# Decay rows of a DeltaNet kept as one DRAM row per head and direction, with their loads and the S5 input store on ScalarE's queue

## The chip, the cores and the metric

The kernel runs on one core of a Trainium2 chip. A core has TensorE (matmuls; its weight loads are shown apart, as PEld), VectorE (DVE), ScalarE (ACT), GpSimd (POOL) and SyncE (SP). Each takes its instructions strictly in order, and they wait for each other on semaphores. DMA transfers are issued as instructions of an engine's queue, here mostly SP's and some ScalarE's; sixteen DMA engines then move the data. [...] 

The metric is the time of one execution on the device in microseconds (us), the median of the runs. The profile is of one execution.

## The reference

One inference step of a hybrid backbone: two layers (DEPTH = 2), 512 latent and 128 context tokens (640 in all), width 1024, float32. Each layer normalises its input, projects it once, and splits the columns among three mixers: a long convolution (Hyena), a diagonal state space model (S5) and a gated DeltaNet with 8 heads of 128 x 128 state in both directions. Each output is gated and projected, the three are merged, and the result is added to the input. Cut to the part whose data the change moves, the DeltaNet takes the tokens in chunks:

```python
gc = jnp.cumsum(g, axis=-1)                       # log decays, within a chunk
diff = gc[..., :, None] - gc[..., None, :]
decay = jnp.where(lower, jnp.exp(jnp.where(lower, diff, 0.0)), 0.0)
a_mat = jnp.where(strict, jnp.einsum('bhncd,bhnsd->bhncs', kb, k) * decay, 0.0)
t_mat = lax.linalg.triangular_solve(a_mat + eye, ...)    # the inverse
...
qk = jnp.where(lower, jnp.einsum('bhncd,bhnsd->bhncs', q, k) * decay, 0.0)
...
    v_new = u_i - jnp.einsum('bhcd,bhdv->bhcv', w_i, S)
    o = (jnp.einsum('bhcd,bhdv->bhcv', q_i * jnp.exp(g_i)[..., None], S)
         + jnp.einsum('bhcs,bhsv->bhcv', qk_i, v_new))
```

The kernel does this in five blocks of 128 tokens; `a_mat` is its tile `N`, `qk` its tile `Pm`. For `decay`, every head and direction needs the row of `gc` of its 640 tokens on all 128 partitions, against the column of each partition.

## The kernel before

Activations are kept transposed: channels on partitions, 640 tokens along the row. Every float32 matmul is done as three faster ones on operands that are split in a high and a low part: `split` (L68) makes `wh` with a cast on ScalarE (L69) and `wl` with a subtraction on VectorE or GpSimd (L70), and `mm3` (L87) runs the three products (L91). `load_w` (L77) loads a 128 x 512 piece of weights, `wr`, on SP (L81), a few pieces ahead. TensorE's projections go on as long as `wr`, `wh` and `wl` arrive in time.

`run` goes over the two layers. In a layer come the norm, then S5 in eight column blocks and the Hyena convolution side by side, then the DeltaNet (`gdn`, L1026), then the merge. Matmuls of gates (results `pg`, sums `gst`, stored to `gt`) are spread between as filler.

S5, `s5_in` (L834): the projection of a block is copied to `u` by ScalarE (L844, L845), stored to the DRAM tile `us` (L846), and read back in another layout by eight loads `U<-us` (L882), which TensorE uses at L908.

DeltaNet: `gdn_scalars` (L1071) computes the running log decays `gc`, 128 tokens x (5 blocks x 16), turns them into `gr` with 80 rows of 128 (L1126), row b * 16 + c for block b and head and direction c, and stores them to the DRAM tile `gcd` (L1127). Then the eight heads go in pairs. `gdn_front` (L1132) projects q, k and v of a head through the gated convolution (`gx`, `gy`, `QT`, `KT`), and makes `kn` and `v`. `gdn_pairs` (L1195) loads, for each of two directions, the 640 values of g of its head onto all 128 partitions (L1202, tile `Pm`, 320 KB), five VectorE operations subtract the column (L1206, through the helper at L138), ScalarE takes the exponential (L1207), and the products with k k and q k follow on VectorE (`N`, `Pm`). `gdn_inverse` (L1313) inverts the triangular `N` of two heads in a chain of VectorE steps (`lt`, `Yl`, L1335 and L1336) and builds `YD`, `YT`, `YB`, `Y1T` from it. `gdn_scan` (L1230) runs the chunks; TensorE reads `Pm` there last (L1253).

Two pools of two buffers each hold `Pm`, so four heads are in work: at a layer's DeltaNet start eight loads of `Pm` come in one burst, after that groups of four.

The order of the instructions on each engine is set when the kernel is built: a scheduler with a simulated timeline picks the next ready instruction from all loops. Where a DMA is issued, what it waits for and how long the simulation takes it to last all enter, so an edit of a DMA can move other instructions.

Of the kernel before, what the change touches and what calls it, by code (L numbers as in the profile page):

```python
# [12 lines left out]
F32 = mybir.dt.float32  # L13
# [39 lines left out]
def bc(ap, shape):  # L53
    return ap.to_broadcast(shape)


class Net:
# [776 lines left out]
    def s5_in(self, l, ct, p, T):  # L834

        nc, a = self.nc, self.a
# [5 lines left out]
        u = p.tile([128, 8, 82], F32, name="u", tag="ys")  # L842
        nc.gpsimd.memset(u[:, :, 64:82:17], 0.0)
        nc.scalar.copy(u[:, :, 0:64], Pu[:, 0:NLAT].rearrange("p (j t) -> p t j", t=8))  # L844
        nc.scalar.copy(u[:, :, 65:81], Pu[:, NLAT:].rearrange("p (j t) -> p t j", t=8))  # L845
        nc.sync.dma_start(T["us"][ct * 128:(ct + 1) * 128], u)  # L846

        ld = {}
        for n in ("sbr", "sbi"):
# [176 lines left out]
    def gdn(self, l, P):  # L1026
        tc, nc, a = self.tc, self.nc, self.a
        self.q2 = self.proj_pools(P, "n", nc.gpsimd, NPM)
        self.pm = P(name="pmb", bufs=NPU, space=PSUM)

        pa = P(name="gda", bufs=1)
        ph = [P(name="gdb", bufs=2)]
        cp = self.gcp
        c = cp.tile([128, 2, 128], F32, name="c6")
        nc.sync.dma_start(c, a["c128"][:, 384:].rearrange("p (n c) -> p n c", n=2))
        self.tri = c
        self.gcw = cp.tile([128, 24, 3], F32, name="gcw")
        nc.scalar.dma_start(self.gcw, a["gcw"][l].rearrange("p (n c) -> p n c", n=24))
        self.ngh = cp.tile([128, 1], F32, name="ngh")
        nc.scalar.dma_start(self.ngh, a["gng"][l])  # L1040
        self.gcd = self.dp.tile([80, 128], F32, name="gcd%d" % l)
        with self.pool(name="gdt", bufs=1) as p:
            self.gdn_scalars(l, cp, p)
        pi = P(name="gdi", bufs=1)
        ph.append(P(name="gdd", bufs=2))
        p = P(name="gdp", bufs=1)

        def front(h):
            return [self.gdn_front(l, h + i, pa, ph[h // 2 % 2]) for i in range(2)]

        def pairs(h, f):
            for i in range(2):
                self.gdn_pairs(h + i, ph[h // 2 % 2], f[i])

        self.LD = pi.tile([128, 32, 32], F32, name="LD")
        nc.gpsimd.memset(self.LD, 0.0)
        self.Y1 = None
        f = front(0)
        pairs(0, f)
        for h in range(0, 8, 2):  # L1060
            self.gdn_inverse(pi, f)
            self.gdn_scan(l, h, p, f)
            if h < 6:
                f = front(h + 2)
                pairs(h + 2, f)
# [5 lines left out]
    def gdn_scalars(self, l, cp, p):  # L1071

        nc, a = self.nc, self.a
        raw = p.tile([128, KT, 32], F32, name="wbr")
        nc.sync.dma_start(raw, a["wba"][l].rearrange("p (k c) -> p k c", k=KT))
        wh = p.tile([128, KT, 32], F32R, name="wbh")
        wl = p.tile([128, KT, 32], F32R, name="wbl")
        self.split(wh, wl, raw)
        ba = p.tile([32, NTOK], F32, name="ba")
        for h in range(2):  # L1080
            s = slice(h * 320, h * 320 + 320)
            P = self.half()
            for kh in range(2):
                self.mark = self.mm3(P[:32], kh, wh[:, 4 * kh:4 * kh + 4], wl[:, 4 * kh:4 * kh + 4], self.hh, self.hl, s, m=32)
            nc.scalar.copy(ba[:, s], P[:32])
        pt = self.half(512)
        for b in range(5):
            self.tr(pt[:, b * 32:b * 32 + 32], ba[:, b * 128:(b + 1) * 128])
        bt = p.tile([128, 5, 32], F32, name="bt")
        nc.vector.tensor_copy(bt, pt[:, :160].rearrange("p (b c) -> p b c", b=5))  # L1090
        al = p.tile([128, 16], F32, name="alog")
        nc.scalar.dma_start(al, bc(a["alog"][l], [128, 16]))
        nc.gpsimd.tensor_tensor(al, self.ebase[:, :16], al, op=ALU.pow)
        dtb = p.tile([128, 16], F32, name="dtb")
        nc.scalar.dma_start(dtb, bc(a["dtb"][l], [128, 16]))
        sh = [128, 5, 16]
        T = lambda n: p.tile(sh, F32, name=n)
        C = lambda n: cp.tile(sh, F32, name=n)
        beta = C("beta")
        nc.scalar.activation(beta, bt[:, :, 0:16], AF.Tanh, scale=0.5)  # L1100
        self.ts(nc.vector, beta, beta, 0.5, 0.5)
        x, ax, g = T("gx"), T("gax"), T("gg")
        nc.vector.tensor_tensor(x, bt[:, :, 16:32], bc(dtb.unsqueeze(1), sh), op=ALU.add)

        nc.scalar.activation(ax, x, AF.Abs)
        nc.scalar.activation(ax, ax, AF.Tanh, scale=0.5)
        self.ts(nc.vector, ax, ax, 0.5, 0.5)
        nc.scalar.activation(ax, ax, AF.Ln)
        self.stt(x, x, 0.0, ax, ALU.max, ALU.subtract)
        self.stt(g, x, -1.0, bc(al.unsqueeze(1), sh))  # L1110
        pc = self.half(512)
        for d in range(2):
            nc.tensor.matmul(pc[:, d * 40:d * 40 + 40], self.tri[:, d, :], g[:, :, d * 8:d * 8 + 8], start=True, stop=True)
        nc.tensor.matmul(pc[:, 128:208], self.ones, g, start=True, stop=True)
        gc = C("gc")
        for d in range(2):
            nc.vector.tensor_copy(gc[:, :, d * 8:d * 8 + 8], pc[:, d * 40:d * 40 + 40].rearrange("p (b c) -> p b c", b=5))
        tot = pc[:, 128:208].rearrange("p (b c) -> p b c", b=5)
        egl, dec, neg, pos = C("egl"), C("dec"), C("neg"), C("pos")
        nc.scalar.activation(egl, tot, AF.Exp)  # L1120
        nc.vector.tensor_tensor(dec, tot, gc, op=ALU.subtract)
        nc.scalar.activation(dec, dec, AF.Exp)
        pr = self.half(512)
        self.tr(pr[:80, :128], gc.rearrange("p b c -> p (b c)"))
        gr = p.tile([80, 128], F32, name="gr")
        nc.scalar.copy(gr, pr[:80, :128])  # L1126
        nc.sync.dma_start(self.gcd, gr)  # L1127
        nc.scalar.activation(pos, gc, AF.Exp)
        self.ts(nc.vector, neg, pos, -1.0)
        self.gs = dict(beta=beta, egl=egl, dec=dec, neg=neg, pos=pos, gc=gc)  # L1130
# [64 lines left out]
    def gdn_pairs(self, h, p, x):  # L1195

        nc, G, KT, QT = self.nc, self.gs, x["KT"], x["QT"]

        Pm = p.tile([128, 2, 5, 128], F32, name="Pm")
        Ed = [Pm[:, d] for d in range(2)]  # L1200
        for d, E in enumerate(Ed):
            nc.sync.dma_start(E, bc(self.gcd.rearrange("(b c) i -> c b i", b=5)[d * 8 + h:d * 8 + h + 1],  # L1202
                                    [128, 5, 128]))
            for b in range(5):
                g = G["gc"][:, b, d * 8 + h:d * 8 + h + 1]
                self.ts(nc.vector, E[:, b, :], E[:, b, :], g, g, ALU.min, ALU.subtract)  # L1206
            nc.scalar.activation(E, E, AF.Exp)  # L1207
        N = p.tile([128, 2, 5, 128], F32, name="N")
        for b0 in (0, 2, 4):
            pb = self.half(512)  # L1210
            n = min(2, 5 - b0)
            pv = pb[:, :n * 256].rearrange("p (x b c) -> p x b c", x=2, b=n)
            for b in range(n):
                t = slice((b0 + b) * 128, (b0 + b) * 128 + 128)
                nc.tensor.matmul(pv[:, 0, b, :], KT[:, t], KT[:, t], start=True, stop=True)
                nc.tensor.matmul(pv[:, 1, b, :], KT[:, t], QT[:, t], start=True, stop=True)
            for d in range(2):
                for b in range(n):
                    self.stt(N[:, d, b0 + b, :], pv[:, 0, b, :], x["sk"][:, b0 + b, d:d + 1], Ed[d][:, b0 + b, :])
                nc.vector.tensor_tensor(Pm[:, d, b0:b0 + n, :], pv[:, 1], Ed[d][:, b0:b0 + n, :], op=ALU.mult)  # L1220

        nc.gpsimd.memset(N[64:128, 0, :, 0:64], 0.0)
        nc.gpsimd.memset(N[0:64, 1, :, 64:128], 0.0)
        for q in (0, 64):
            nc.gpsimd.memset(N[q + 32:q + 64, 0, :, q:q + 32], 0.0)
            nc.gpsimd.memset(N[q:q + 32, 1, :, q + 32:q + 64], 0.0)
        nc.gpsimd.tensor_tensor(Pm, Pm, bc(self.tri.unsqueeze(2), [128, 2, 5, 128]), op=ALU.mult)
        x.update(N=N, Pm=Pm)
# [470 lines left out]
```

## Time and profile before

| | |
|---|---|
| median of 3 runs | 3738.56 us (3723.69 to 3741.91) |
| profiled execution | 3732.11 us |
| its span, first to last instruction | 3730.3 us |
| mean granted TensorE clock | 0.95 |
| TensorE busy | 3380.0 us, 91% of the span |
| VectorE, GpSimd, ScalarE busy | 64%, 52%, 38% |
| `Pm<-gcd` loads | 32 of 320 KB, landing after 11.0 us (median) |
| `us<-u` stores | 16 of 328 KB, landing after 4.2 us (median) |

Engine rows read thus: time, engine, line, operation, output tile <- input tiles, shape, how many alike. In square brackets stands how long the engine was idle just before, and whose end released it. A duration with SPq is the time for which SP was busy issuing, not the transfer; the transfer's end is the landing. Busy time of a matmul is modelled from its issue, and at the lower clock the same matmul takes longer, so a stretch is judged by busy time and granted clock together.

### The profile page before, as it was taken

To read this page: it belongs to the slowest core of one execution; us is meant where nothing else is said; L and a number is where in the kernel's file an instruction comes from. 1 tells how busy PE (TensorE), PEld (TensorE's weight loads), DVE (VectorE), ACT (ScalarE), POOL (GpSimd) and SP (SyncE) were. 2 spreads that over 40 slices of the span, in tenths; PEclk is the share of its full clock that TensorE was granted. 3 is DMA by queue.
4 is the path that set the end of the run, shared out by engine and by line. 5 is a ranking of instruction groups with operands and counts; after the bars stand their busy time and mean duration, and the time that the engine had idled before them with its cause. 6 is when DMAs were issued, how large, how long until landed. Compare 5 with 4: busy or idle time off the path is not lost. (4 is left out here: it accounts for less than half of the span.)

```text
span 3730.3 us, 68509 instructions
## 1 busy us (share of the span) xinstructions
PE 3380.0 (91%) x25850; PEld 3220.4 (86%) x25850; DVE 2369.6 (64%) x4615; ACT 1413.4 (38%) x3295; POOL 1942.9 (52%) x2153
## 2 busy tenths in 40 slices
PE   6899898999979898899979999999989898898998
PEld 5798878888979887799978889988889898797998
DVE  6777677777227873743747776677773378875354
ACT  4433232332244445443334333323322545445422
POOL 4777777776345443401336777878763544341010
PEclk7999899999989998999989999999999999899999
DMA  6322334322232212533633222233222322134352
GB/s 242 110 73 82 94 107 115 108 73 63 78 93 65 68 62 68 170 126 109 188 113 98 75 71 83 81 75 81 76 66 77 92 64 78 41 97 139 125 178 89
DMA packets 310602, 363.05 MB, mean 97 GB/s; under 512 B 86814, under 2 KB 190270, under 8 KB 310016
## 3 DMA queue, kind: packets, MB, share of 16 engines
q1 hardware_dynamic: 305368, 358.01, 32.6%
q8 instruction: 204, 3.34, 0.4%
q10 hardware_dynamic: 4904, 0.66, 0.1%
q14 instruction: 126, 1.03, 0.1%
HBM read 291.87 MB, written 66.67 MB: 96 GB/s over the span
## 5 line engine op out<-in xcount | busy, mean ns | idle before, releaser
L91 PE MATMUL pj<-hh,wh 128*128 128x320 f32 x2048 | 666.4, 326 | 60.5 <-ACT wh L69 32.2
L91 PE MATMUL pj<-hh,wl 128*128 128x320 f32 x2048 | 655.5, 322 | 10.5 <-DVE wl L70 8.0
L91 PE MATMUL pj<-hl,wh 128*128 128x320 f32 x2048 | 657.9, 321 | 5.5 <-DVE hl L70 5.4
L70 POOL TENSOR_TENSOR wl<-wr,wh 128x512 fp32r<-128x512 f32 x288 | 392.1, 1365 | 448.9 <-ACT wh L69 388.7
L69 ACT CAST wh<-wr 128x512 fp32r<-128x512 f32 x608 | 374.8, 618 | 659.7 <-PE pj L91 486.3
L91 PEld LDWEIGHTS pj<-hh,wh 128*128 128x128 f32 x2048 | 400.7, 196 | 70.8 <-ACT wh L69 33.6
L91 PE MATMUL pg<-hh,wh 128*128 128x320 f32 x1280 | 415.1, 325 | 15.2 <-ACT wh L69 10.5
L91 PE MATMUL pg<-hh,wl 128*128 128x320 f32 x1280 | 407.6, 323 | 9.3 <-POOL wl L70 9.2
L70 DVE TENSOR_TENSOR wl<-wr,wh 128x512 fp32r<-128x512 f32 x320 | 259.5, 812 | 244.4 <-ACT wh L69 243.1
L91 PEld LDWEIGHTS pj<-hh,wl 128*128 128x128 f32 x2048 | 398.8, 195 | 14.9 <-DVE wl L70 9.3
L91 PE MATMUL pg<-hl,wh 128*128 128x320 f32 x1280 | 411.5, 322 | 0.0
L91 PEld LDWEIGHTS pj<-hl,wh 128*128 128x128 f32 x2048 | 400.3, 195 | 11.1 <-DVE hl L70 8.8
L91 PE MATMUL pj<-yh,wh 128*128 128x320 f32 x1024 | 318.0, 312 | 6.5 <-ACT yh L69 5.1
L91 PE MATMUL pj<-yl,wh 128*128 128x320 f32 x1024 | 318.9, 312 | 2.6 <-DVE yl L70 2.5
L91 PE MATMUL pj<-yh,wl 128*128 128x320 f32 x1024 | 317.5, 311 | 0.0
L91 PEld LDWEIGHTS pg<-hh,wh 128*128 128x128 f32 x1280 | 250.4, 196 | 19.4 <-ACT wh L69 11.6
L91 PEld LDWEIGHTS pg<-hh,wl 128*128 128x128 f32 x1280 | 247.4, 194 | 14.2 <-POOL wl L70 12.5
L91 PEld LDWEIGHTS pg<-hl,wh 128*128 128x128 f32 x1280 | 249.5, 195 | 0.9 <-issue 0.4
L91 PEld LDWEIGHTS pj<-yh,wh 128*128 128x128 f32 x1024 | 193.4, 189 | 8.1 <-ACT yh L69 5.9
L91 PEld LDWEIGHTS pj<-yl,wh 128*128 128x128 f32 x1024 | 193.5, 189 | 4.8 <-DVE yl L70 4.8
L91 PEld LDWEIGHTS pj<-yh,wl 128*128 128x128 f32 x1024 | 193.6, 189 | 0.0
L1514 POOL TENSOR_TENSOR m<-m,gt 128x640 f32<-128x640 f32 x16 | 31.1, 1943 | 295.8 <-DVE gt L132 295.8
(523 smaller groups left out, 8673.3 us busy)
## 6 DMA issues: line engine op xcount, KB each, us to landing
wr<-in_wt SPq DMA_DIRECT2D x608, 256.0 KB, 2.7
gt<-gst SPq DMA_DIRECT2D x160, 160.0 KB, 2.0
gt<-gt SPq DMA_DIRECT2D x64, 320.0 KB, 3.4
wr<-in_wmod SPq DMA_DIRECT2D x64, 256.0 KB, 3.3
Pm<-gcd SPq DMA_DIRECT2D x32, 320.0 KB, 11.0
wm<-in_wmod SPq DMA_DIRECT2D x4, 2048.0 KB, 16.8
M<-ks SPq DMA_DIRECT2D x256, 32.0 KB, 1.8
us<-u SPq DMA_DIRECT2D x16, 328.0 KB, 4.2
```

Of the source, the lines that this page charges most:

```text
L69: self.nc.scalar.copy(h, src)
L70: (eng or self.nc.vector).tensor_tensor(l, src, h.bitcast(F32), op=ALU.subtract)
L91: ins = self.nc.tensor.matmul(o, w[:, k, :m], x[:, kh * 4 + k, s], start=kh == 0 and k == 0 and i == 0, stop=kh == 1 and k == 3 and i == 2)
L1514: nc.gpsimd.tensor_tensor(m[i], m[i], g, op=ALU.add)
```

## The change

There are three edits. The S5 input store (L846) is issued from ScalarE's queue and not from SP's. The DRAM tile `gcd` gets the shape 16 x 5 x 128, so that the 640 values of one head and direction lie in one row of 2560 bytes; the store at L1127, still on SP, writes its 80 rows of 512 bytes to their new places. The 32 loads at L1202 read such a row as one run for each partition, where they read five runs of 512 bytes that lay 8 KB apart, and they are issued from ScalarE's queue.

```diff
--- before.py
+++ after.py
@@ -843,7 +843,7 @@
         nc.gpsimd.memset(u[:, :, 64:82:17], 0.0)
         nc.scalar.copy(u[:, :, 0:64], Pu[:, 0:NLAT].rearrange("p (j t) -> p t j", t=8))
         nc.scalar.copy(u[:, :, 65:81], Pu[:, NLAT:].rearrange("p (j t) -> p t j", t=8))
-        nc.sync.dma_start(T["us"][ct * 128:(ct + 1) * 128], u)
+        nc.scalar.dma_start(T["us"][ct * 128:(ct + 1) * 128], u)
 
         ld = {}
         for n in ("sbr", "sbi"):
@@ -1038,7 +1038,7 @@
         nc.scalar.dma_start(self.gcw, a["gcw"][l].rearrange("p (n c) -> p n c", n=24))
         self.ngh = cp.tile([128, 1], F32, name="ngh")
         nc.scalar.dma_start(self.ngh, a["gng"][l])
-        self.gcd = self.dp.tile([80, 128], F32, name="gcd%d" % l)
+        self.gcd = self.dp.tile([16, 5, 128], F32, name="gcd%d" % l)
         with self.pool(name="gdt", bufs=1) as p:
             self.gdn_scalars(l, cp, p)
         pi = P(name="gdi", bufs=1)
@@ -1124,7 +1124,7 @@
         self.tr(pr[:80, :128], gc.rearrange("p b c -> p (b c)"))
         gr = p.tile([80, 128], F32, name="gr")
         nc.scalar.copy(gr, pr[:80, :128])
-        nc.sync.dma_start(self.gcd, gr)
+        nc.sync.dma_start(self.gcd.rearrange("c b i -> b c i"), gr)
         nc.scalar.activation(pos, gc, AF.Exp)
         self.ts(nc.vector, neg, pos, -1.0)
         self.gs = dict(beta=beta, egl=egl, dec=dec, neg=neg, pos=pos, gc=gc)
@@ -1199,8 +1199,7 @@
         Pm = p.tile([128, 2, 5, 128], F32, name="Pm")
         Ed = [Pm[:, d] for d in range(2)]
         for d, E in enumerate(Ed):
-            nc.sync.dma_start(E, bc(self.gcd.rearrange("(b c) i -> c b i", b=5)[d * 8 + h:d * 8 + h + 1],
-                                    [128, 5, 128]))
+            nc.scalar.dma_start(E, bc(self.gcd[d * 8 + h:d * 8 + h + 1], [128, 5, 128]))
             for b in range(5):
                 g = G["gc"][:, b, d * 8 + h:d * 8 + h + 1]
                 self.ts(nc.vector, E[:, b, :], E[:, b, :], g, g, ALU.min, ALU.subtract)
```

The lines below the edit at L1202 are one lower in the changed kernel (the exponential is at L1206, `N` copies at L1380).

ScalarE at the DeltaNet start of layer 0, from the copy that fills the stored rows on; `wh<-wr` is the weight cast, `gx<-pj` a projection's copy. Before:

```order
L1126 COPY gr<-pj 80x128
L69 CAST wh<-wr 128x512
L1147 COPY gx<-pj 128x320
L1207 ACTIVATE Pm<-Pm 128x640
L69 CAST wh<-wr 128x512
L1147 COPY gx<-pj 128x320
```

After:

```order
L1126 COPY gr<-pj 80x128
L1202 DMA Pm<-gcd_10377 128x640 x3
L69 CAST wh<-wr 128x512
L1202 DMA Pm<-gcd_10377 128x640 x3
L1147 COPY gx<-pj 128x320
L1202 DMA Pm<-gcd_10377 128x640 x2
L1206 ACTIVATE Pm<-Pm 128x640
L69 CAST wh<-wr 128x512
```

The eight loads stand among the casts and copies; the exponentials and casts keep their order.

SP at the same place; `wr<-in_wt` are weight loads, `gt<-gst` stores of gates. Before:

```order
L81 DMA wr<-in_wt 128x512
L1127 DMA gcd_10377<-gr 80x128
L1202 DMA Pm<-gcd_10377 128x5x128 x8
L81 DMA wr<-in_wt 128x512 x3
L1425 DMA gt_496<-gst 128x320
```

After:

```order
L81 DMA wr<-in_wt 128x512
L1127 DMA gcd_10377<-gr 5x16x128
L81 DMA wr<-in_wt 128x512 x3
L1424 DMA gt_496<-gst 128x320
L81 DMA wr<-in_wt 128x512 x4
```

The weight loads follow the store directly, and the store's outermost size is 5 where it was 80.

VectorE at the last group of four loads in layer 1, around the first operations on `Pm`; `YD`, `YT`, `YB`, `Y1T` and `N` are tiles of the inverse of the heads in work, `S` and `os` of the scan, `fac` of the output gate. Before:

```order
L1185 TENSOR_TENSOR kn<-pj,dec 128x512 x2
L138 TENSOR_SCALAR fac<-fac 128x5
L1336 TENSOR_TENSOR Yl<-Yl,lt 128x31
L138 TENSOR_SCALAR Pm<-Pm,gc 128x128 x5
L1257 COPY S_32709<-pb 128x128
L138 TENSOR_SCALAR Pm<-Pm,gc 128x128
L1342 STREAM_TRANSPOSE YD<-Yl 128x1024
L138 TENSOR_SCALAR Pm<-Pm,gc 128x128 x2
```

After:

```order
L1352 STREAM_TRANSPOSE YB<-YD 128x160
L1351 STREAM_TRANSPOSE YT<-YD 128x160
L1352 STREAM_TRANSPOSE YB<-YD 128x160
L1270 TENSOR_TENSOR os_32461<-os_32461,pb 128x128
L1380 COPY N<-YB 32x10x32 x2
L1374 COPY Y1T<-YT 32x10x32 x4
L1380 COPY N<-YB 32x10x32 x6
L1185 TENSOR_TENSOR kn<-pj,dec 128x512 x2
L138 TENSOR_SCALAR Pm<-Pm,gc 128x128 x3
```

Before, the operations on `Pm` stand ahead of the transpose `YD`; after, `YD` and all that is made from it stand ahead of them. TensorE's own order is the same over most of layer 1; in layer 0's S5 and Hyena stage rows have moved by up to a hundred places.

## Rows read from the trace of the kernel before

**Rows 1.** Page, part 1: busy us, share of the span, instructions of each engine.

```profile
PE 3380.0 (91%) x25850; PEld 3220.4 (86%) x25850; DVE 2369.6 (64%) x4615; ACT 1413.4 (38%) x3295; POOL 1942.9 (52%) x2153
```

**Rows 2.** Windows: length, busy PE, PEld, DVE, ACT, POOL; PEclk, DMA share, GB/s.

```profile
1025.00:1055.00 30.00, 13.04 (x56) 12.12 (x55) 12.05 (x42) 10.47 (x17) 5.45 (x5) 0.66 0.44 106
1285.00:1300.00 15.00, 8.55 (x43) 8.55 (x44) 10.85 (x28) 9.27 (x17) 5.16 (x6) 0.77 0.53 118
1420.00:1450.00 30.00, 16.35 (x98) 14.95 (x102) 9.89 (x37) 12.90 (x25) 9.40 (x10) 0.71 0.36 99
2885.00:2915.00 30.00, 19.33 (x100) 18.54 (x100) 13.70 (x44) 15.79 (x24) 6.76 (x6) 0.77 0.54 128
3120.00:3145.00 25.00, 17.25 (x87) 15.88 (x85) 16.12 (x53) 11.55 (x32) 7.92 (x9) 0.73 0.42 116
3240.00:3265.00 25.00, 14.58 (x76) 13.68 (x75) 17.74 (x53) 12.12 (x26) 8.39 (x10) 0.69 0.36 85
100.00:950.00 850.00, 774.35 (x6035) 721.03 (x6035) 609.07 (x975) 271.77 (x762) 632.73 (x740) 0.95 0.34 91
1950.00:2800.00 850.00, 789.02 (x5872) 750.38 (x5871) 605.88 (x907) 281.81 (x768) 644.49 (x736) 0.97 0.30 79
```

**Rows 3.** Line L1202: issue ns min/median/max, who waited for it (us, times), landing.

```profile
L1202 SPq DMA_DIRECT2D Pm<-gcd x32: 371/517/4936, 1017.6 to 3245.9; - x32
...
  DVE Pm L138: 86.8, 23
...
DMA to landing us min/median/max: 7.8/11.0/15.4
```

**Rows 4.** Timeline of SP at both DeltaNet starts: start us, us, what.

```profile
1017.61 18.59 SPq L1202 DMA_DIRECT2D Pm<-gcd  x8
1036.30 15.77 SPq L81 DMA_DIRECT2D wr<-in_wt  x3
...
2878.61 14.32 SPq L1202 DMA_DIRECT2D Pm<-gcd  x8
2893.02 13.55 SPq L81 DMA_DIRECT2D wr<-in_wt  x3
```

**Rows 5.** Timeline of TensorE, 1025 to 1055 us, the two longest waits.

```profile
1030.12 0.63 PE L91 MATMUL pj<-hh,wh 128*128 128x320 f32 x1 [3.78 <-ACT wh L69]
...
1050.40 0.63 PE L91 MATMUL pj<-hh,wh 128*128 128x320 f32 x1 [12.74 <-ACT wh L69]
```

**Rows 6.** Timeline of ScalarE, same stretch.

```profile
1028.82 0.74 ACT L1207 ACTIVATE Pm<-Pm 128x640 f32<-128x640 f32 x1 [8.76 <-DVE Pm L138]
...
1049.73 0.62 ACT L69 CAST wh<-wr 128x512 fp32r<-128x512 f32 x1 [9.61 <-DMA wr<-in_wt]
```

**Rows 7.** Timeline of VectorE, 1420 to 1450 us, the two longest waits.

```profile
1422.94 0.60 DVE L138 TENSOR_SCALAR Pm<-Pm,gc 128x128 f32<-128x128 f32 x2 [7.35 <-DMA Pm<-gcd]
...
1442.18 1.37 DVE L138 TENSOR_SCALAR Pm<-Pm,gc 128x128 f32<-128x128 f32 x5 [9.38 <-DMA Pm<-gcd]
```

**Rows 8.** Chain that ended last, 3120 to 3260 us: start us, us, step.

```profile
3131.66 9.34 DMA Pm<-gcd
```

**Rows 9.** Line L1506, loads of `m` in the merge: issue ns, landing us.

```profile
L1506 SPq DMA_DIRECT2D m<-md x16: 320/430/997, 1641.9 to 3453.4; - x16
...
DMA to landing us min/median/max: 3.0/6.1/7.3
```

**Rows 10.** Page, part 6: DMA issues, KB each, us to landing.

```profile
fg<-in_fg SPq DMA_DIRECT2D x1, 512.0 KB, 4.1
...
gcd<-gr SPq DMA_DIRECT2D x2, 40.0 KB, 1.5
```

**Rows 11.** Line L695, loads that ScalarE issues: issue ns min/median/max.

```profile
L695 ACTq DMA_DIRECT2D stp<-in_ls x4: 473/473/487, 45.3 to 1795.2; - x4
```

**Rows 12.** Line L846, the S5 input store: landing.

```profile
DMA to landing us min/median/max: 2.2/4.2/8.8
```

**Rows 13.** Line L882, loads of the S5 input: who waited (us, times).

```profile
  PE pb L908: 12.8, 5
```

## The prediction

> **What bounds the kernel now.** I read the busy times first. TensorE is busy for 3380.0 of 3730.3 us, no other engine for more than 64% [rows 1], so the end moves only where TensorE gets work sooner. Next I cut the span into stretches and took for each its length less TensorE's busy time multiplied by its granted clock share: the time lost to gaps and to the slow clock together. Over 1950 to 2800 us that is 850 - 789.02 x 0.97 = 85 us, about 1 us in 10; it is the kernel's usual level. Six stretches are much worse, and in all six the Decay rows (tile Pm) are being loaded [rows 2]:
>
> | stretch, us | lost | usual | excess |
> |---|---|---|---|
> | 1025 to 1055 (GDN start, layer 0) | 30 - 13.04 x 0.66 = 21.4 | 3.0 | 18.4 |
> | 2885 to 2915 (GDN start, layer 1) | 30 - 19.33 x 0.77 = 15.1 | 3.0 | 12.1 |
> | 1285 to 1300 | 15 - 8.55 x 0.77 = 8.4 | 1.5 | 6.9 |
> | 1420 to 1450 | 30 - 16.35 x 0.71 = 18.4 | 3.0 | 15.4 |
> | 3120 to 3145 | 25 - 17.25 x 0.73 = 12.4 | 2.5 | 9.9 |
> | 3240 to 3265 | 25 - 14.58 x 0.69 = 14.9 | 2.5 | 12.4 |
>
> The excess is 75.1 us: 30.5 at the two starts, 44.6 in the four middle stretches. That is all there is to win near these loads.
>
> Then I asked what is late there. The 32 Pm loads land 7.8 to 15.4 us after issue, median 11.0; VectorE waits for them 86.8 us in 23 places [rows 3]. At a GDN start SP spends 18.59 us (layer 1: 14.32) issuing eight of them, and the three weight loads queued behind take another 15.77 (13.55) [rows 4]. The effect on TensorE is two gaps, 3.78 us and 12.74 us, both ended by the cast `wh` [rows 5]. The two have different causes. The first cast stands in ScalarE's queue behind the exponential of the first Pm, which waited 8.76 us for VectorE; the second waited 9.61 us for the weight load itself [rows 6]. In the middle stretches (four loads each) VectorE stands still, 7.35 and 9.38 us in the worst one [rows 7], and two such loads lie on the chain that ended last, one with 9.34 us [rows 8].
>
> **The change part by part.**
>
> *The load's shape.* A load reads 128 runs of 2560 B where it read 640 runs of 512 B. No such Pm load is in the trace. The nearest rows are the loads of `m`, also 128 runs of 2560 B and eight in a row: 320 to 997 ns to issue, landing after 3.0 to 7.3 us, median 6.1 [rows 9]. One broadcast load with long runs, `fg`, has 512 KB and lands after 4.1 us [rows 10], so that reading one row for all partitions need not be slow. I take 3 to 7 us where there were 11.0.
>
> *GDN starts.* With SP free after the store, the three weight loads go out some 18.6 us sooner; in ScalarE's row the casts lie between the Pm issues, and only one exponential is ahead of the second of them. If the loads go out at about 1017 us and the first lands 3 to 7 us later, that exponential and the cast behind it are done by 1022 to 1026; TensorE ran out at 1030.12 - 3.78 = 1026.3 [rows 5]. Both gaps close. I take the whole excess: 30.
>
> *Middle stretches.* From 11.0 to between 6.1 and 3.0 a wait loses 45% to 73%; I take 59% of 44.6, which is 26. The floor is the VectorE work itself: it is idle for only 15 - 10.85 = 4.2, 25 - 16.12 = 8.9 and 25 - 17.74 = 7.3 us of three of these stretches, and for 20.1 of the fourth [rows 2]. Together 40.5, so 26 fits under it. The order helps here: in the last group VectorE now does the transposes and the copies of `N` before the first Pm operation, which covers part of a landing.
>
> *ScalarE issues.* It gets 32 + 16 more DMA issues; its own now take 473 ns [rows 11], so 32 x 0.45 = 14.4 us for Pm. The 16 at the starts stand ahead of TensorE's reserve worked out above and are hidden. The 16 in the middle (7.2) stand in ScalarE's queue ahead of `gx`, `v` and `wh`, where ScalarE is also waited for; I put half on the path: 4. Each first load of a head must also wait, in ScalarE's order, until TensorE has read the old Pm of that slot; queued behind it are the same casts and copies. The order puts other ScalarE work in front, so 1 us in all, between 0 and 5. Sum: 5.
>
> *The store of the rows.* `gcd<-gr` landed in 1.5 us [rows 10]. It still writes 80 runs of 512 B, but in another order. From the row itself, 0 more; from the S5 store with eight times its bytes, median 4.2 [rows 12], 2.7 more at each start. Most of it lies before 1026.3, so I take 1 for both. [...] No run so far shows this store.
>
> *The S5 store.* TensorE waits for the S5 input's loads 12.8 us in five places [rows 13]; the store's issue leaves SP, where weight and gate loads stood before it, and follows the copies that fill it on ScalarE. At best that returns 12.8. Against it stand 16 issues x 0.47 = 7.5 us on ScalarE, idle there for two thirds of the time (281.81 busy of 850 [rows 2]). I take 4 gained.
>
> *Reordering.* The planner has also moved other work of layer 0's S5 and Hyena stage by up to a hundred rows. That stage loses 850 - 774.35 x 0.95 = 114 us over 100 to 950, against 85 in layer 1's like stretch [rows 2], a third apart for the same work; so I allow 10 us either way and take 0.
>
> *Sum:* 30 + 26 - 5 - 1 + 4 = 54 us. Against the profiled execution, 3732.1 us (span 3730.3), that gives 3678. The median of the runs shown is 3738.6, 6.5 above it; I forecast against the median: **3684.6 us**, within 3666 and 3708 (the store's bound, reordering, and 45% to 73%).
>
> **The rivals.**
>
> *The loads don't become shorter, and ScalarE inherits the queue (slower).* If the cost is the broadcast itself, eight loads still take 18.59 us to issue, now on ScalarE, 2.3 us each, up to 4.9 [rows 3, 4]. At the starts the second cast then comes as late as before, and nothing is won: 0. In the middle 16 x 2.3 = 37 us hold the engine that makes `wh` and `gx`; half on the path is 18, the slot waits 5, reordering 5: 28 slower, about 3767. It decides where landings stay above about 9 us and an issue takes over 1 us. For it: so far every Pm load shows this. Against it: `fg`, and `m` with the same runs. [...] Chance 0.06.
>
> *Only the starts are won.* In the middle stretches the wait for the slot, the ScalarE issues, or VectorE's own chain takes the place of the landing: 26 falls away, leaving 30 - 5 - 1 = 24 and so 3715; with reordering at its bad end 3725. For it: three middle stretches have VectorE idle for under 9 us. Against it: the two loads on the chain that ended last. Chance 0.22, half of it within 0.5%.
>
> *Nearly everything is won.* All 75.1 and the 12.8 of the S5 loads: 3738.6 - 88 = 3651. It needs landings at 3 us and VectorE never late. Chance 0.13.
>
> *Nothing moves.* The gaps close, but TensorE then waits at the same places for VectorE's inverse or for weights. Chance 0.01 beside the half above.
>
> **How the numbers follow.** Forecast 0.58, everything 0.13, only the starts 0.22, nothing 0.01, slower 0.06. This kernel's measurement can tell about 0.5% from no change, that is 3720 to 3757. Faster: 0.58 + 0.13 + 0.11 = 0.82; same 0.12; slower 0.06. The range leaves out the slower rival, the lower part of everything-won and the upper part of the starts alone: 3650 to 3722.
>
> **What the changed kernel's profile would show.** Pm landings of 3 to 7 us and issues under 0.6 us on ScalarE's queue; VectorE's wait for them down from 86.8 to under 25; SP going from the store straight to weight loads; TensorE's busy share in the two starts like the rest of the kernel. [...] The forecast is wrong if issues on ScalarE take over 1 us, if ScalarE stands before a Pm load for several us, or if the middle stretches still lose over 15 us more than usual in all with short landings.

## The result, and the profile after

The changed kernel takes 3643.87 us (median, 3638.89 to 3651.86), the kernel before 3737.82 us beside it. The ratio is 0.9757, 95% interval 0.9726 to 0.9788: 91 us or 2.4% faster. The forecast of 3684.6 us had the direction right and the size wrong; the time lies 22 us under the first range that the prediction gives (3666 to 3708) and 6 us under the second (3650 to 3722). The profiled execution took 3638.9 us with a span of 3637.1, 93.2 less than [rows 1] came from.

First the page's part 1 of the changed kernel (busy us, share of the span, instructions):

```profile
PE 3347.8 (92%) x25850; PEld 3198.3 (88%) x25850; DVE 2371.0 (65%) x4615; ACT 1414.8 (39%) x3295; POOL 1948.5 (54%) x2153
```

The same 25850 matmuls are busy for 32.2 us less than in [rows 1], and the mean granted clock rose from 0.950 to 0.958. The clock records of the two traces hold two shares only, 1.0 and 0.5, and the lower one for 372.4 us before and 305.2 after. At a share of 0.51 a 128x320 matmul of L91 took 0.47 us (before, 1050 to 1054 us), at 1.00 it took 0.31 (1054 to 1058). The other 61 us are idle time that is gone. Line L1202 of the changed kernel (issue ns min/median/max, who waited and for how long, landing):

```profile
L1202 ACTq DMA_DIRECT2D Pm<-gcd x32: 326/390/1166, 1018.2 to 3172.9; - x32
...
  DVE Pm L138: 19.5, 5
  ACT L1206: 0.8, 1
...
DMA to landing us min/median/max: 3.3/3.7/7.9
```

Against [rows 3] the landing went from 11.0 to 3.7 us, VectorE's wait from 86.8 to 19.5, and no issue takes over 1.2 us. The trace holds the landing of 22 of the 32 loads before and of 17 after, so the two medians are of unlike sets; the first load of layer 1's start, which it holds in both, went from 7.8 to 3.5 us. At the start of layer 0's DeltaNet, SP goes from the store straight to the weight loads (against [rows 4]):

```profile
1015.71 0.86 SPq L1127 DMA_DIRECT2D gcd<-gr  x1
1021.54 11.32 SPq L81 DMA_DIRECT2D wr<-in_wt  x3
```

Its first load of the three goes out 14.8 us earlier than the first in [rows 4]. The trace puts SP's wait of 4.9 us ahead of it down to a landing of `Pm`, and of the 11.32 us of the row 6.3 us to `wl` (L70) on GpSimd, which reads `wr`, and 3.5 to a landing of `wr`. ScalarE there (in brackets the idle time before, and what ended it), to be held against [rows 6]:

```profile
1018.16 1.30 ACTq L1202 DMA_DIRECT2D Pm<-gcd  x3
1019.50 0.62 ACT L69 CAST wh<-wr 128x512 fp32r<-128x512 f32 x1 [4.05 <-PE pj L91]
1019.53 1.38 ACTq L1202 DMA_DIRECT2D Pm<-gcd  x3
1020.95 0.43 ACT L1147 COPY gx<-pj 128x320 f32<-128x320 f32 x1 [0.83 <-PE pj L91]
1020.98 0.92 ACTq L1202 DMA_DIRECT2D Pm<-gcd  x2
1023.10 0.74 ACT L1206 ACTIVATE Pm<-Pm 128x640 f32<-128x640 f32 x1 [1.73 <-DVE Pm L138]
1023.75 0.60 ACT L69 CAST wh<-wr 128x512 fp32r<-128x512 f32 x1
```

The eight issues take 3.6 us in all and the second cast comes at 1023.75, before 1026.3, where TensorE ran out in the kernel before [rows 5]. The two gaps of [rows 5] are gone; what comes next is a shorter one, 5.54 us, at TensorE, behind `gx` on ScalarE, which now has all eight exponentials (0.74 us each) and two table loads (1.28 us each) between 1023.10 and 1041.05:

```profile
1048.65 2.30 PE L1165 MATMUL pj<-c,gx 128*128 128x2 f32 x10 [5.54 <-ACT gx L1162]
```

Where the 93 us went, by stage. A stage at a DeltaNet start is from the copy `gr` to the first `YD` of the layer, the middle from there to the last load of `m`; S5 and Hyena of layer 1 run from the copy `u` of its second column block to `gr`:

| stage | before | after | difference |
|---|---|---|---|
| DeltaNet start, layer 0 | 156.9 | 140.5 | -16.4 |
| middle groups, layer 0 | 474.6 | 440.1 | -34.5 |
| S5 and Hyena, layer 1 | 918.4 | 913.5 | -4.9 |
| DeltaNet start, layer 1 | 148.5 | 141.5 | -7.0 |
| middle groups, layer 1 | 428.1 | 397.6 | -30.5 |
| all else | 1603.8 | 1603.9 | +0.1 |

The middle groups give 65 of the 93 us. Their windows, layer 0 and layer 1 before, then after (columns as in [rows 2]):

```profile
1171.30:1645.90 474.60, 423.58 (x3719) 403.68 (x3718) 307.95 (x824) 236.84 (x553) 175.80 (x188) 0.95 0.30 92
3025.30:3453.40 428.10, 380.02 (x3353) 360.44 (x3353) 300.73 (x824) 216.79 (x517) 156.08 (x174) 0.92 0.28 87
```

```profile
1155.70:1595.80 440.10, 410.46 (x3721) 394.81 (x3720) 307.44 (x824) 234.92 (x551) 175.89 (x188) 0.98 0.31 99
2962.60:3360.20 397.60, 368.07 (x3339) 350.58 (x3339) 297.75 (x824) 216.64 (x517) 157.16 (x173) 0.94 0.29 92
```

The worst place of before was around 1420 us. Here is a stretch of 60 us around that group of four loads, first before, then after; in both kernels it begins 19 us before the first of the four is issued:

```profile
1394.00:1454.00 60.00, 42.94 (x319) 40.57 (x318) 22.22 (x68) 30.68 (x73) 20.92 (x21) 0.77 0.32 91
```

```profile
1368.00:1428.00 60.00, 57.26 (x606) 55.50 (x606) 31.52 (x88) 39.03 (x93) 22.76 (x23) 0.97 0.27 85
```

Before, 60 - 42.94 x 0.77 = 26.9 us were lost in it, after 60 - 57.26 x 0.97 = 4.5.

### The profile page after: what moved, and what is told of

Its sections match the earlier page's. It is cut to its first block, busy times and chain, and to the rows that moved or that the text cites. A ratio compares the mean times of both kernels' runs of the same rounds, so it can differ in the third digit from the quotient of the medians.

```text
span 3637.1 us, 68480 instructions
## 1 busy us (share of the span) xinstructions
PE 3347.8 (92%) x25850; PEld 3198.3 (88%) x25850; DVE 2371.0 (65%) x4615; ACT 1414.8 (39%) x3295; POOL 1948.5 (54%) x2153
## 4 chain that ended last, share of the span: by engine, by line
PE 47%; DVE 18%; POOL 11%; issue 8%; DMA 3%; ACT 2%; SPq 1%; POOLq 0%; DVEq 0%; ACTq 0%
PE pj L91 21%; PE pg L91 10%; DVE lt L1334 2%; DVE Yl L1335 2%; PE pb L129 1%; POOL Y L669 1%; POOL et L830 1%; POOL wl L70 1%; PE pb L659 1%; PE pb L661 1%; POOL E L829 1%; DVE R L939 1%; PE pb L997 1%; PE pb L908 1%; POOL E L831 1%
## 5 line engine op out<-in xcount | busy, mean ns | idle before, releaser
L91 PE MATMUL pj<-hh,wh 128*128 128x320 f32 x2048 | 656.4, 321 | 28.3 <-ACT hh L69 17.6
L91 PE MATMUL pj<-hl,wh 128*128 128x320 f32 x2048 | 652.9, 319 | 5.6 <-DVE hl L70 5.5
L91 PE MATMUL pj<-hh,wl 128*128 128x320 f32 x2048 | 649.9, 318 | 2.4 <-POOL wl L70 2.2
L70 POOL TENSOR_TENSOR wl<-wr,wh 128x512 fp32r<-128x512 f32 x288 | 394.2, 1372 | 380.9 <-ACT wh L69 340.8
L91 PEld LDWEIGHTS pj<-hh,wh 128*128 128x128 f32 x2048 | 393.4, 192 | 37.0 <-ACT hh L69 19.8
L91 PE MATMUL pg<-hh,wh 128*128 128x320 f32 x1280 | 417.7, 327 | 7.0 <-ACT gst L1423 3.4
L70 DVE TENSOR_TENSOR wl<-wr,wh 128x512 fp32r<-128x512 f32 x320 | 252.5, 791 | 253.9 <-ACT wh L69 252.4
L91 PE MATMUL pg<-hh,wl 128*128 128x320 f32 x1280 | 411.6, 326 | 6.0 <-POOL wl L70 6.0
L91 PE MATMUL pg<-hl,wh 128*128 128x320 f32 x1280 | 412.3, 323 | 0.0
L91 PEld LDWEIGHTS pj<-hl,wh 128*128 128x128 f32 x2048 | 393.1, 192 | 11.1 <-DVE hl L70 8.8
L91 PEld LDWEIGHTS pj<-hh,wl 128*128 128x128 f32 x2048 | 392.4, 192 | 5.9 <-POOL wl L70 3.5
L91 PE MATMUL pj<-yl,wh 128*128 128x320 f32 x1024 | 318.0, 311 | 2.5 <-DVE yl L70 2.2
L91 PE MATMUL pj<-yh,wh 128*128 128x320 f32 x1024 | 317.0, 312 | 2.0 <-ACT yh L69 1.2
L91 PE MATMUL pj<-yh,wl 128*128 128x320 f32 x1024 | 316.9, 310 | 0.0
L91 PEld LDWEIGHTS pg<-hh,wh 128*128 128x128 f32 x1280 | 252.4, 197 | 9.8 <-ACT wh L69 5.3
L91 PEld LDWEIGHTS pg<-hh,wl 128*128 128x128 f32 x1280 | 249.1, 196 | 10.7 <-POOL wl L70 9.2
L91 PEld LDWEIGHTS pg<-hl,wh 128*128 128x128 f32 x1280 | 252.0, 197 | 0.9 <-issue 0.4
L91 PEld LDWEIGHTS pj<-yl,wh 128*128 128x128 f32 x1024 | 193.2, 189 | 4.0 <-DVE yl L70 4.0
L91 PEld LDWEIGHTS pj<-yh,wh 128*128 128x128 f32 x1024 | 192.6, 189 | 3.5 <-ACT yh L69 2.2
L91 PEld LDWEIGHTS pj<-yh,wl 128*128 128x128 f32 x1024 | 193.1, 189 | 0.0
```

Source lines behind the costliest of these rows:

```text
L70: (eng or self.nc.vector).tensor_tensor(l, src, h.bitcast(F32), op=ALU.subtract)
L91: ins = self.nc.tensor.matmul(o, w[:, k, :m], x[:, kh * 4 + k, s], start=kh == 0 and k == 0 and i == 0, stop=kh == 1 and k == 3 and i == 2)
```

## Experiments

Theory 1: the shape of the load (128 long runs where there were 640 short ones) carries the gain. Theory 2: ScalarE's queue carries it. Theory 3: the planner's new order does (the planner is the scheduler that fixes every engine's order when the kernel is built). Ratios are to the kernel before in the same session.

| kernel | median us | ratio | 95% interval |
|---|---|---|---|
| changed kernel | 3643.87 | 0.9757 | 0.9726 to 0.9788 |
| rows_sp: row layout, loads and S5 store on SP | 3666.37 | 0.9829 | 0.9807 to 0.9851 |
| pad640: changed, 640 runs 640 B apart | 3654.93 | 0.9799 | 0.9775 to 0.9824 |
| old_act: old layout, loads on ScalarE's queue | 3724.93 | 0.9994 | 0.9977 to 1.0011 |
| us_act: S5 store alone | 3725.98 | 0.9988 | 0.9976 to 1.0000 |
| before_s17: before, blocks 8704 B apart | 3670.95 | 0.9832 | 0.9817 to 0.9846 |
| after_8k: changed, 640 runs 8 KB apart | 3753.68 | 1.0046 | 1.0027 to 1.0064 |
| rows_act: row layout, loads on ScalarE's queue | 3654.01 | 0.9791 | 0.9773 to 0.9808 |
| rows_sp_us: row layout on SP, S5 store on ScalarE's | 3659.23 | 0.9799 | 0.9784 to 0.9814 |
| rows_sp_n1: rows_sp, order disturbed | 3665.76 | 0.9817 | 0.9802 to 0.9832 |
| after_n1: changed, order disturbed | 3647.65 | 0.9772 | 0.9754 to 0.9790 |

Two more, after_4k (3711.82) and after_2k (3681.92), are single runs. Of each of these kernels the table's time is a median of 4 to 10 runs.

### The parts alone

rows_sp, against the changed kernel:

```diff
-            nc.scalar.dma_start(E, bc(self.gcd[d * 8 + h:d * 8 + h + 1], [128, 5, 128]))
+            nc.sync.dma_start(E, bc(self.gcd[d * 8 + h:d * 8 + h + 1], [128, 5, 128]))
...
-        nc.scalar.dma_start(T["us"][ct * 128:(ct + 1) * 128], u)
+        nc.sync.dma_start(T["us"][ct * 128:(ct + 1) * 128], u)
```

> The row layout alone: gcd as one row per head and direction, the 32 loads still on SP's queue, the S5 store still on SP. VectorE's and ScalarE's order is almost that of the kernel before. Theory 1 (the shape of the load is the cause: 128 long runs land early and are quickly issued): landings 3 to 8 us, nearly the whole gain, about 3655 us. Theory 2 (ScalarE's queue, which frees SP for weight loads, carries the gain): gaps at the DeltaNet starts remain, about 3715. Theory 3 (the planner's new order carries the larger part of the middle groups' gain): landings short, starts closed, but the middle groups win only what their waits lost, 45 to 50 us in all, about 3690.

Landings were 3.4 to 7.6 us, median 3.8. The layout alone gives 1.7% or 64 us, some two thirds of the whole. A small part of that may be order, since 344 of VectorE's 4615 instructions stand at another place in its trace than in that of before. Its profile has the starts as in the changed kernel (-16.3 and -5.8 us) and -28.3 and -15.3 us in the middle groups: 43.6, where the prediction called 44.6 excess, 22.3 in each layer.

old_act, against the kernel before:

```diff
-            nc.sync.dma_start(E, bc(self.gcd.rearrange("(b c) i -> c b i", b=5)[d * 8 + h:d * 8 + h + 1],
+            nc.scalar.dma_start(E, bc(self.gcd.rearrange("(b c) i -> c b i", b=5)[d * 8 + h:d * 8 + h + 1],
```

> The old layout (640 runs of 512 B), the 32 loads issued from ScalarE's queue, the S5 store on SP. Theory 1: landings stay near 11 us, no gain, between 3735 and 3770. Theory 2: SP free for weight loads, 30 us of the starts won, about 3700 to 3710. Theory 3: the order is close to that of the kernel before, so about 3735.

No difference that can be measured. Theory 2 falls: with slow loads (median landing 10.3 us) the queue brings nothing, and ScalarE is held by the issues. Lines of its L1202:

```profile
L1202 ACTq DMA_DIRECT2D Pm<-gcd x32: 366/514/4936, 1021.1 to 3242.1; - x32
...
  DVE Pm L138: 85.0, 24
  ACT gx L1147: 20.7, 2
...
DMA to landing us min/median/max: 7.8/10.3/16.5
```

VectorE waits as in [rows 3], and ScalarE's copies `gx` now wait 20.7 us behind the issues.

us_act, against the kernel before:

```diff
-        nc.sync.dma_start(T["us"][ct * 128:(ct + 1) * 128], u)
+        nc.scalar.dma_start(T["us"][ct * 128:(ct + 1) * 128], u)
```

> The S5 input store alone moved to ScalarE's queue; decay rows as before. All theories: TensorE's waits for the S5 loads fall from 12.8 to about 5 us, so 3730 to 3735; the planner's order changes by more than with the layout alone, so theory 3 allows up to 20 us either way.

About 4 us, at the edge of what the interval can tell. TensorE's wait for the S5 loads fell from 12.8 [rows 13] to 6.6 us. That wait scatters from kernel to kernel: 7.7 to 12.8 us in the six with the store on SP, 2.1 to 7.5 in the eight with it on ScalarE's queue.

### Number of runs, or their distance

pad640, against the changed kernel:

```diff
-        self.gcd = self.dp.tile([16, 5, 128], F32, name="gcd%d" % l)
+        self.gcd = self.dp.tile([16, 5, 160], F32, name="gcd%d" % l)
...
-            nc.scalar.dma_start(E, bc(self.gcd[d * 8 + h:d * 8 + h + 1], [128, 5, 128]))
+            nc.scalar.dma_start(E, bc(self.gcd[d * 8 + h:d * 8 + h + 1, :, :128], [128, 5, 128]))
```

> The changed kernel with each 128-value piece of a row padded to 160 values in DRAM, so that a load reads 640 runs of 512 B again, 640 B apart; queues and the order of every engine's instructions are those of the changed kernel. Theory 1: landings 8 to 15 us again, issues on ScalarE of over 1 us at the starts, the gain gone: 3735 or slower, to 3770. Theory 2 and theory 3: most of the gain stays, 3660 to 3680. If the distance between the runs (8 KB before) and not their number were the cost: landings under 5 us and about 3645.

The store at L1127 is fitted to the padded tile in the same way. Theory 1, as it was put, falls: with 640 runs of 512 B the loads still land after 3.3 to 7.6 us, and most of the gain stays.

```profile
L1202 ACTq DMA_DIRECT2D Pm<-gcd x32: 366/469/2592, 1018.0 to 3187.5; - x32
...
  DVE Pm L138: 24.4, 10
...
DMA to landing us min/median/max: 3.3/4.6/7.6
```

The number of runs may be worth the rest, 0.9799 against 0.9757: some 16 us, with overlapping intervals and an uncertainty of about as much. Issues took up to 2.6 us on ScalarE, where they took up to 1.2. The distance was left: runs of the old layout lie exactly 8 KB apart. Two kernels put that to the test from both sides. before_s17, against the kernel before, adds one row that nobody uses to each block of 16:

```diff
-        self.gcd = self.dp.tile([80, 128], F32, name="gcd%d" % l)
+        self.gcd = self.dp.tile([5, 17, 128], F32, name="gcd%d" % l)
...
-        nc.sync.dma_start(self.gcd, gr)
+        nc.sync.dma_start(self.gcd[:, :16, :], gr)
...
-            nc.sync.dma_start(E, bc(self.gcd.rearrange("(b c) i -> c b i", b=5)[d * 8 + h:d * 8 + h + 1],
+            nc.sync.dma_start(E, bc(self.gcd.rearrange("b c i -> c b i")[d * 8 + h:d * 8 + h + 1],
```

> The kernel before with one unused row added to each block of 16 rows, so that a load's five runs of 512 B lie 8704 B apart instead of 8192; loads and S5 store stay on SP. The order of VectorE and ScalarE is that of rows_sp. Theory A (the padded kernel showed that 640 near runs land as early as 128 long ones, so the cause is that runs exactly 8 KB apart collide): landings 3 to 5 us, time as rows_sp, about 3665. Theory B (nearness matters: runs within 3 KB are cheap, runs some KB apart are not): landings near 11 us, time as before, about 3730.

```profile
L1202 SPq DMA_DIRECT2D Pm<-gcd x32: 370/517/2252, 1021.4 to 3197.2; - x32
...
  DVE Pm L138: 25.5, 10
...
DMA to landing us min/median/max: 3.4/4.3/7.2
```

Theory A holds: the same 640 runs on the same queue, only 8704 instead of 8192 bytes apart, land after 4.3 instead of 11.0 us [rows 3], and the kernel takes as long as rows_sp, whose order it has on VectorE and ScalarE, with its 128 long runs. On SP the number of runs is worth nothing that can be measured (0.9832 and 0.9829); whether the 16 us above come from issues that hold ScalarE is not shown. after_8k is pad640 with 2048 values in place of 160, so that the runs are 8 KB apart in the changed kernel; the order of all engines is that of the changed kernel:

> The changed kernel with each 128-value piece of a row padded to 2048 values, so that a load reads five runs of 512 B exactly 8 KB apart; the order of all engines and the queues are those of the changed kernel. Theory A (runs 8 KB apart collide) and theory B (far runs are slow): landings 8 to 15 us and the gain of the faster load gone. If the early landing is all the gain: 3725 to 3760, with ScalarE held by issues. If the planner's order and ScalarE's queue carry a third of it: about 3700. If the landing stays under 5 us, the number and the distance of the runs are both innocent and only the old place of the rows is left: about 3650.

It is slower than the kernel before, and 110 us slower than the changed kernel with the same order. So the new order does not carry the gain by itself (theory 3), and the gain is lost where the loads are slow. L1202, then ScalarE at the first DeltaNet start:

```profile
L1202 ACTq DMA_DIRECT2D Pm<-gcd x32: 366/527/9053, 1020.7 to 3283.9; - x32
...
  DVE Pm L138: 128.1, 28
  ACT gx L1147: 41.7, 2
...
DMA to landing us min/median/max: 7.6/13.1/21.8
```

```profile
1020.72 1.54 ACTq L1202 DMA_DIRECT2D Pm<-gcd  x3
1022.31 0.62 ACT L69 CAST wh<-wr 128x512 fp32r<-128x512 f32 x1 [4.48 <-issue]
1022.33 20.96 ACTq L1202 DMA_DIRECT2D Pm<-gcd  x3
1043.33 0.43 ACT L1147 COPY gx<-pj 128x320 f32<-128x320 f32 x1 [20.40 <-DMA Pm<-gcd]
```

Three issues hold ScalarE for 20.96 us, where three took 1.38 in the changed kernel. This is the wait that the prediction's slower rival described, though with landings longer than before (13.1 us against 11.0). after_4k and after_2k have 1024 and 512 values in place of 160:

> The changed kernel with pieces of a row 4 KB apart, order and queues unchanged. If runs collide only where they are 8 KB apart: landings as with 640 B, median near 4.6 us, about 3655. If collisions come with any large power of two: median 7 us or more, and 3680 to 3755.

> The same with 2 KB. Near 4.6 us and 3655 if the collision needs 4 or 8 KB; between the two otherwise.

Landings, first 4 KB and then 2 KB:

```profile
DMA to landing us min/median/max: 6.1/7.7/21.3
```

```profile
DMA to landing us min/median/max: 4.8/6.9/14.5
```

With these the time rises step by step with the distance: 3655 (640 B), 3682, 3712, 3754 us (8 KB), the two in the middle from one run each. It needs no exact 8 KB, and distance alone is not it, since 8704 B is quick. Only 2, 4 and 8 KB were tried as slow distances; whether 6 KB, say, is slow too no run shows.

### What ScalarE's queue adds

rows_act is the changed kernel with the S5 store back on SP, rows_sp_us the one with the loads back on SP.

> Row layout and loads on ScalarE's queue, S5 store still on SP. The layout with SP gave 3666, the full change 3644. If ScalarE's queue for the loads makes the remaining difference: about 3645. If it is the S5 store, or an order that only both together bring: about 3665.

> Row layout with the loads on SP, and the S5 store on ScalarE's queue. Alone the store gave about 4 us. If effects simply add: 3666 - 4 = 3662. If the S5 store (and the planner's order that comes with it) makes the remaining difference to the full change: about 3645.

Neither of them explains the rest alone: on top of the layout the loads' queue gives about 14 us (0.9829 to 0.9791), the S5 store's about 11 (0.9829 to 0.9799), each with an uncertainty of about 10, and both together 27 (0.9829 to 0.9757). To see whether that is luck of the planner's order, two tiny loads of constants were moved between queues, in rows_sp and in the changed kernel:

```diff
-        nc.scalar.dma_start(al, bc(a["alog"][l], [128, 16]))
+        nc.sync.dma_start(al, bc(a["alog"][l], [128, 16]))
...
-        nc.scalar.dma_start(dtb, bc(a["dtb"][l], [128, 16]))
+        nc.sync.dma_start(dtb, bc(a["dtb"][l], [128, 16]))
```

> Row layout with loads and S5 store on SP (3666 before), and two tiny loads of constants at the DeltaNet start (a log and dt bias, issued once a layer) moved from ScalarE's queue to SP's, which by themselves cost nothing that shows: a disturbance of the planner's order. If the last 12 and 11 us that ScalarE's queue brought for the loads and for the S5 store are luck of the order, such a disturbance moves the time by as much, 3650 to 3680. If they belong to the queue: 3661 to 3671.

> The same disturbance (two tiny constant loads from ScalarE's queue to SP's) of the changed kernel. Luck of the order: 3644 moves by 10 us or more, mostly up. The queue's own gain: 3639 to 3649.

The order moves (601 and 525 of VectorE's 4615 instructions stand at another place in the traces; between rows_sp and rows_act it is 1004), the medians by 1 and 4 us, the ratios by 0.12% and 0.15%. In these two trials a disturbance does not give or take 20 us, and the step between the disturbed pair is 0.9817 to 0.9772, 17 us. That speaks for the queue, but it does not clear the order. Take the last stage of the DeltaNet in layer 1, from the last `YD` to the last load of `m`. It starts at least 100 us after the last load of `Pm`, so no load of the decay rows is in flight. That stage of rows_sp, of old_act, of the changed kernel and of after_n1:

```profile
3291.06:3387.58 96.52, 84.11 (x747) 78.54 (x746) 52.66 (x140) 49.58 (x120) 9.85 (x8) 0.93 0.46 145
```

```profile
3357.89:3446.18 88.29, 77.79 (x723) 71.34 (x722) 51.50 (x130) 46.77 (x109) 8.71 (x7) 0.98 0.46 151
```

```profile
3276.46:3360.16 83.70, 77.14 (x726) 71.65 (x725) 49.72 (x125) 46.06 (x105) 7.48 (x6) 0.98 0.47 158
```

```profile
3270.58:3368.57 97.99, 84.92 (x763) 79.04 (x763) 56.73 (x144) 50.87 (x125) 10.02 (x8) 0.91 0.42 139
```

It is 8 us shorter in old_act, whose loads are slow, and 13 us shorter in the changed kernel, with some twenty matmuls fewer in it. In after_n1, whose loads are quick and on ScalarE's queue, it is as long as in rows_sp, and yet the whole kernel takes only some 5 us more than the changed one. So the planner's order shifts ten us and more between stages, and the length of one stage does not tell what the order is worth to the whole. How much of the 27 us is order and how much the queue itself stays open, since no kernel here has one order with either queue.

## Why the prediction was right or wrong

*What bounds the kernel.* Right in the main: the time was lost where the decay rows are loaded, by gaps and by the lower clock beside them, and it came back there. Around the gap of 12.74 us in [rows 5] the granted share is 0.50 from 1042 to 1050 us, within the gap, 0.51 from 1050 to 1054 and 1.00 from 1054 to 1062. The 75.1 us were not all there was to win there, though: the starts and the middle groups gave 23.4 + 65.0 = 88.4.

*The load's shape.* The number was right (3 to 7 us forecast, 3.3 to 7.9 measured, median 3.7), the reason was mostly not. I put it down to 128 long runs instead of 640 short ones. With 640 runs at another distance the median landing is 4.3 to 4.6 us; it was the 8 KB between the runs that made 11.0. The rows of `m` and `fg` that I took for comparison differ from the old load in both respects, so they could not tell the two apart.

*GDN starts.* 30 forecast, 23.4 measured (16.4 + 7.0). Both gaps of layer 0 closed by the steps named; what was missed is the next wait, 5.54 us for `gx` in layer 0, where ScalarE's exponentials now crowd.

*Middle stretches.* This is the step that failed: 26 forecast, 65 measured. I scaled the loss with the landing (59% of 44.6). rows_sp, with short landings and almost the order of before, returned 43.6, so about the whole excess came back and not 59% of it. The likely reason is that a wait does not scale with the landing: where the data is there before VectorE asks, the whole wait is gone (VectorE waited in 23 places before and in 5 in the changed kernel), and the clock beside it is higher (0.77 before and 0.97 after in the stretch shown). That the sum comes so near to 44.6 is partly luck, since 28.3 came back in layer 0 and 15.3 in layer 1, for 22.3 in each. The stretches were also cut too narrow: around 1420 us 26.9 - 4.5 = 22.4 came back, where I had counted 15.4 as excess. The other 21 of the 65 came only with the loads and the S5 store on ScalarE's queue. For these I had a cost of 5 and a gain of 4, and no term for what the queue, or the order that comes with it, would return in the middle groups; which of the two it was stays open. The idle time of VectorE, which I used as a floor, was no floor: 65 is more than its 40.5.

*ScalarE issues.* -5 forecast; with fast loads the loads' queue gave about +14, and how much of that is order stays open. The duration was right (0.39 us each, median), though one issue took 1.17 us, over the 1 us that I had named as a sign of being wrong. The cover was better than half: of ScalarE's own work only 0.8 us in all waited behind these loads.

*The store of the rows.* About 1 forecast, between 0 and 1 measured. The store itself, before and after:

```profile
L1127 SPq DMA_DIRECT2D gcd<-gr x2: 340/382/423, 1014.8 to 2877.1; - x2
```

```profile
L1127 SPq DMA_DIRECT2D gcd<-gr x2: 800/828/857, 1015.7 to 2821.4; - x2
```

Its issue takes twice as long, 828 ns against 382 (median). The first load reads what it stored; in layer 1 of the kernel before it went out 1.51 us after the store's issue, and the store landed after 1.5 [rows 10]. In the changed kernel it went out 2.30 us after the store's issue there, and in layer 0 18.16 minus 15.71 = 2.45 us after it, where it was 2.76. The landing of the store itself has no row after. The first range of the prediction counts in a bound for this store that no run shows; in its place they showed these 2.45 and 2.30 us.

*The S5 store.* +4 forecast; alone about 4, on top of the layout about 11 with an uncertainty of 10. TensorE's wait, 12.8 before [rows 13], from line L882 after:

```profile
  PE pb L908: 5.1, 5
```

*Reordering.* Zero was right for the stage that I looked at: that of layer 0 is 0.8 us longer. The bound of 10 us was fair, since rows_act's profile is 11 us longer there. The order within the DeltaNet, which shifts ten us and more between its stages, I did not price.

*The rivals.* "Nearly everything is won" came nearest, 3651 forecast and 3644 measured, with a chance of 0.13. In part that is luck, because its parts were off in opposite ways: the starts gave 23.4 for 30.5, the middle groups 65 for 44.6, and layer 1's S5 and Hyena stage 4.9, where 12.8 had been put down for the S5 loads of both layers. Of its conditions the short landings came (median 3.7 us); VectorE is still late by 19.5 us in five places. "Only the starts" had it the wrong way round, since the middle gave most. The slower rival's premise, slow loads on ScalarE's queue, is old_act, and the 28 us that I had worked out are not there (0.9994). after_8k, whose landings are longer than those of before and hold ScalarE, is 17 us slower than before.

## What to carry to other kernels

Look at the addresses of a DMA before its size: where many partitions read the same few runs, runs 2, 4 or 8 KB apart took 1.5 to 3 times as long to land as the same runs 640 or 8704 B apart (median 6.9 to 13.1 us against 4.3 to 4.6), and one unused row in 17 brought the landing from 11.0 to 4.3 us. If the data will be there before it is asked for, value the wait at its full length, with the lower clock beside it, not in proportion; and cut the stretch wide enough that it holds the clock's recovery (here the share was 0.51 in the 4 us after the gap of 12.74 us, and 1.00 in the next). Move the issue of a load onto a busy engine only once the load is quick: three issues held ScalarE for 20.96 us in after_8k, where the loads land after 13.1 us (median), and for 1.38 us in the changed kernel, where they land after 3.7.

## What the runs showed of the hardware that I had not expected

The landing of a 320 KB load to 128 partitions that reads five runs of 512 B for each depended on the distance of the runs, on either queue:

| kernel | distance of the runs | landing, median and maximum us | longest issue us |
|---|---|---|---|
| pad640 | 640 B | 4.6, 7.6 | 2.6 |
| before_s17 | 8704 B | 4.3, 7.2 | 2.3 |
| after_2k | 2 KB | 6.9, 14.5 | 4.4 |
| after_4k | 4 KB | 7.7, 21.3 | 6.5 |
| before | 8 KB, heads 512 B apart | 11.0, 15.4 | 4.9 |
| old_act | as before, on ScalarE's queue | 10.3, 16.5 | 4.9 |
| after_8k | 8 KB, heads a multiple of 8 KB apart | 13.1, 21.8 | 9.1 |

The data and the number of runs are the same in all seven rows. The figures are of those loads whose landing the trace holds, 13 to 22 of the 32. For one load that all seven hold, the first of layer 1's start, the landing is 3.5, 3.9, 5.1, 7.0, 7.8, 7.8 and 11.1 us in the order of the rows. From old_act to after_8k the runs of one load lie alike and the queue is the same, but the heads lie elsewhere (512 B apart, and 40 KB) and the order differs; that the place of the heads makes the difference is not shown, and what is slow about these distances no row names.
